# Sources of the first FFN pair kept on chip instead of passing through DRAM

## The chip, the core and the metric

The kernel runs on one core of a Trainium2 chip. That core has five engines that run side by side and wait for each other through semaphores: TensorE (PE in the profile, with its weight loads as PEld), VectorE (DVE), ScalarE (ACT), GpSimd (POOL), and SyncE (SP), which here does nothing but issue DMA transfers, one after the other. Each engine works through its own list of instructions in a fixed order; one that has to wait holds up all that stand behind it on its engine. The metric is the time of one execution on the device, in microseconds.

## The reference

One decoder layer on a sequence of 512 tokens with 2048 features, all float32. The part that matters here is its end:

```
x  = x + mix @ w_out                                  # mix: 512 x 2048, w_out: 2048 x 2048
h2 = rms_norm(x, norm2_g)
x  = x + (silu(h2 @ w_gate) * (h2 @ w_up)) @ w_down   # w_gate, w_up: 2048 x 5632
```

Ahead of it stand a normalisation, one combined projection, gated linear attention on four heads and dilated windowed attention on eight; the change touches none of these.

## The kernel before

**Big products.** Every large product, activations times weights, runs in *pairs* of two output column chunks of 512 columns, by a scheme of seven block products for a two-by-two block product. The left factor is the activations, transposed: for a *group* of 512 input features (two blocks of 256) and the two halves of the tokens there are four blocks, r11, r21 (first feature block, token half 0 and 1) and r12, r22 (second feature block). The seven products of a pair use seven left factors of each group: A11 = r11, S1 = r21 + r22, S2 = S1 - r11, S4 = r12 - S2, S3 = r11 - r21, A12 = r12 and A22 = r22 (the table `COMBO`). A pair has four groups (for 2048 input features), so 28 of these left factors, and it runs P1, P5, P6, P3, P7, P2, P4, four groups each, 28 *groups of matmuls* in all.

**Splits.** A float32 product is made of three products of a shorter float type. Of each left factor ScalarE makes a high part (L161, a cast) and VectorE a low part (L162, source minus high part); this is `Operand.split`. The weights are split in the same way, 128 x 1024 at a time: ScalarE casts `wh` (L331), VectorE subtracts to give `wl` (L335). A group of matmuls is eight matmuls on `wh` and then four on `wl`, all at L358. For P5, P6, P7 and P4 the weights are also sums of two quarters, and VectorE makes the sum in place (L256) two groups ahead. For P1, P3 and P2 there is no sum. `wh` and `wl` have two buffers each, so VectorE can make the `wl` of a group only when the matmuls on the `wl` two groups before are done.

**What sets the order.** `stream` walks all pairs and all groups; in each group it emits the casts and subtractions of the next one or two, its matmuls, and between the `wh` and `wl` matmuls it calls `p.step()`. That call runs due *deferred* work (`later(n, fn)`: n calls from now) and then takes one step of the *background* list, which holds generators that build left factors for later pairs. `paced([...])` gives how many background steps each call takes, in order; past the end of the list it is one. The framework then fixes the order of each engine from dependences, buffers and the order of emission, so the places on the engines are not exactly those of the code.

**From w_out to the FFN.** The second pair of `w_out` makes column chunks 2 and 3 of the new x. Its four closing products give them one token half at a time, in the order P3 (chunk 3, token half 1), P7 (chunk 3, half 0), P2 (chunk 2, half 1), P4 (chunk 2, half 0). `final_out` adds the old x (loaded into tiles `q` and `k`, L1192; added at L1194 or L1197), stores the sum for later (L1211), squares it for the norm (L1213) and defers `turn`, which transposes the tile on TensorE (L1019, eight matmuls of 128 x 128), scales it out of PSUM by norm2_g on ScalarE (L1030) into tiles `oT` and `PT`, and stores these to the DRAM tensors `xn_d` (L1034). The row factor of the norm is applied only when the FFN's products leave PSUM (`tok_scale`).

The first FFN pair (weights `w_gate` and `w_up`, columns of j = 0) takes its left factors for groups 0 and 1 from chunks 0 and 1, and for groups 2 and 3 from chunks 2 and 3. For groups 0 and 1 `operand_jobs` loads the turned blocks back from `xn_d` into tiles `r` (L1073) and splits them during the second `w_out` pair. For groups 2 and 3 `early_job` loads r11 and r21 into tiles `top` (L1073) and makes A11 and S3, and `late_jobs` loads blocks again, into `r` (L1073) and `v`, `T`, `qT`, `kT` (L1107), and makes S1, S2 (L1121, L1123), S4 (L1125), A12 and A22. All these left factors stay in SBUF for the 11 FFN pairs. `before_ffn(0)` makes sure that S3 of group 3 has been emitted before the first FFN pair begins; from there the list `paces[0]` places the steps.

## Time and profile before

| what | value |
|---|---|
| three runs | 1965.07 us median, 1964.33 to 1965.67 |
| the profiled execution's own time | 1958.01 us |
| its span, from the first to the last instruction | 1956.1 us |
| mean granted TensorE clock | 0.999 |
| DMA packets of the execution | 158855, 362.52 MB |
| second `w_out` pair, 28 groups | from 642.12 us |
| first FFN pair, 28 groups | from 720.81 us |

The profile is one execution with the profiler on. Busy times of engines are sums over their instructions; since instructions of one engine overlap a little at their ends, the distance from one start to the next is what a row of instructions costs. In the listing of instructions by time a line gives start, duration, engine, line of the code, operation, the tiles (out<-in, buffer numbers left out), how many equal ones were merged, and in square brackets how long the engine had been idle before and who ended that. SPq is SyncE's list of DMA issues: its durations are those of issuing, not of the transfer.

In what follows W0 to W27 are the groups of matmuls of the second `w_out` pair and F0 to F27 those of the first FFN pair; `wl(F1)` is the low weight part of group F1. Groups 4 to 11, 16 to 19 and 24 to 27 of a pair use summed weights.

### The profile page before, as it was taken

The numbers are of one execution on the slowest core, as the hardware profiler recorded it, in microseconds if no ns is written. First come the engines' busy times: TensorE is split into PE (matmuls) and PEld (weight loads), VectorE is DVE, ScalarE is ACT, GpSimd is POOL, SyncE is SP. The second block draws the span as 40 slices with busy tenths as digits, with TensorE's granted clock in tenths as the row PEclk, the third lists the DMA queues.
The fourth block names the chain that finished last, engine by engine and source line by source line (L and its number), as shares of the span: only waits on it lengthen the run. The fifth ranks groups of instructions, "written<-read, shape, count | busy, mean of one in ns | idle before, by whom it ended". The sixth has DMA issues, their size and how long they took to land.

```text
span 1956.1 us, 25599 instructions
## 1 busy us (share of the span) xinstructions
PE 1918.2 (98%) x9160; PEld 1657.3 (85%) x9160; DVE 1648.0 (84%) x1845; ACT 1088.1 (56%) x1580; POOL 55.2 (3%) x73
## 2 busy tenths in 40 slices
PE   8999999999999999999999999999999999999998
PEld 6788888888878888888888888888888888888887
DVE  7996887768789989878878879879879989989977
ACT  9654554667666665544544545545546646546443
POOL 0000330011000000000000000000000000000000
PEclk9999999999999999999999999999999999999999
DMA  9545555444567584453453453443445865855662
GB/s 355 174 154 206 179 173 171 143 156 162 198 217 241 181 289 148 154 188 141 155 183 135 162 182 120 171 171 124 173 170 176 279 212 182 292 198 180 230 215 76
DMA packets 158855, 362.52 MB, mean 185 GB/s; under 512 B 16438, under 2 KB 43359, under 8 KB 158728
## 3 DMA queue, kind: packets, MB, share of 16 engines
q1 hardware_dynamic: 158584, 360.89, 53.1%
q8 instruction: 71, 1.16, 0.2%
q14 instruction: 56, 0.46, 0.1%
q10 hardware_dynamic: 144, 0.01, 0.0%
HBM read 298.68 MB, written 64.51 MB: 186 GB/s over the span
## 4 chain that ended last, share of the span: by engine, by line
PE 75%; DVE 6%; DMA 3%; issue 2%; ACT 1%; SPq 0%; POOL 0%; DVEq 0%; ACTq 0%
PE acc L358 71%; DVE wl L335 2%; PE bank L1019 1%; DVE wa L256 1%; PE bank L926 1%; PE bank L904 1%; DVE AS L162 1%; PE bank L919 0%; DMA xn_d<-PT 0%; DMA q<-y_d 0%; PE bank L895 0%; DMA q<-in_x 0%; DMA T<-p_d 0%; DMA r<-xn_d 0%; ACT wh L331 0%
## 5 line engine op out<-in xcount | busy, mean ns | idle before, releaser
L358 PE MATMUL acc<-wh,AS 128*128 128x512 f32 x3008 | 712.2, 379 | 0.9 <-DVE AS L162 0.8
L358 PEld LDWEIGHTS acc<-wh,AS 128*128 128x128 f32 x3008 | 568.0, 189 | 82.8 <-DVE AS L162 1.6
L331 ACT CAST wh<-wa 128x1024 fp32r<-128x1024 f32 x376 | 394.3, 1049 | 395.1 <-PE acc L358 365.2
L358 PE MATMUL acc<-wh,AA 128*128 128x512 f32 x2256 | 533.7, 379 | 1.1 <-ACT wh L331 0.9
L335 DVE TENSOR_TENSOR wl<-wa,wh 128x1024 fp32r<-128x1024 f32 x376 | 458.7, 1223 | 74.5 <-ACT wh L331 45.6
L358 PEld LDWEIGHTS acc<-wh,AA 128*128 128x128 f32 x2256 | 426.0, 189 | 62.7 <-ACT wh L331 2.3
L358 PE MATMUL acc<-wl,AS 128*128 128x512 f32 x1504 | 395.3, 385 | 7.6 <-DVE wl L335 7.5
L358 PEld LDWEIGHTS acc<-wl,AS 128*128 128x128 f32 x1504 | 279.2, 189 | 61.0 <-DVE wl L335 20.3
L358 PE MATMUL acc<-wl,AA 128*128 128x512 f32 x1128 | 296.1, 385 | 3.4 <-DVE wl L335 3.3
L358 PEld LDWEIGHTS acc<-wl,AA 128*128 128x128 f32 x1128 | 209.3, 189 | 35.8 <-DVE wl L335 7.5
L331 ACT CAST wh<-wb 128x1024 fp32r<-128x1024 f32 x94 | 98.6, 1049 | 123.8 <-PE acc L358 117.1
L331 ACT CAST wh<-wc 128x1024 fp32r<-128x1024 f32 x94 | 98.4, 1047 | 109.2 <-PE acc L358 106.6
L331 ACT CAST wh<-wd 128x1024 fp32r<-128x1024 f32 x94 | 98.6, 1049 | 103.6 <-PE acc L358 98.5
L335 DVE TENSOR_TENSOR wl<-wc,wh 128x1024 fp32r<-128x1024 f32 x94 | 115.0, 1223 | 41.7 <-ACT wh L331 41.7
L335 DVE TENSOR_TENSOR wl<-wd,wh 128x1024 fp32r<-128x1024 f32 x94 | 114.8, 1223 | 37.8 <-ACT wh L331 28.7
L256 DVE TENSOR_TENSOR wa<-wc,wa 128x1024 f32<-128x1024 f32 x94 | 114.8, 1225 | 35.6 <-DMA wc<-in_w_gate 20.8
L335 DVE TENSOR_TENSOR wl<-wb,wh 128x1024 fp32r<-128x1024 f32 x94 | 114.5, 1221 | 5.3 <-ACT wh L331 4.9
L256 DVE TENSOR_TENSOR wa<-wb,wa 128x1024 f32<-128x1024 f32 x94 | 113.8, 1222 | 1.7 <-DMA wb<-in_w_in 1.0
L256 DVE TENSOR_TENSOR wb<-wd,wb 128x1024 f32<-128x1024 f32 x94 | 114.8, 1223 | 0.4
L256 DVE TENSOR_TENSOR wa<-wd,wa 128x1024 f32<-128x1024 f32 x94 | 113.5, 1223 | 0.1
L298 DVE SCALAR_TENSOR_TENSOR seed<-acc,rs,seed 128x512 f32<-128x512 f32 x96 | 70.5, 747 | 27.6 <-PE acc L358 27.5
L282 ACT ACTIVATE seed<-acc,rs 128x512 f32<-128x512 f32 x96 | 60.8, 682 | 3.1 <-PE acc L358 3.1
(285 smaller groups left out, 1332.2 us busy)
## 6 DMA issues: line engine op xcount, KB each, us to landing
wa<-in_w_gate SPq DMA_DIRECT2D x44, 512.0 KB, 3.4
wb<-in_w_up SPq DMA_DIRECT2D x44, 512.0 KB, 4.0
wd<-in_w_up SPq DMA_DIRECT2D x44, 512.0 KB, 4.1
wc<-in_w_gate SPq DMA_DIRECT2D x44, 512.0 KB, 3.4
wc<-in_w_in SPq DMA_DIRECT2D x28, 512.0 KB, 3.5
wa<-in_w_in SPq DMA_DIRECT2D x24, 512.0 KB, 4.9
wb<-in_w_in SPq DMA_DIRECT2D x24, 512.0 KB, 5.7
wd<-in_w_in SPq DMA_DIRECT2D x24, 512.0 KB, 5.1
```

Of the source, the lines that this page charges most:

```text
L162: nc.vector.tensor_tensor(a[:, :, 1, :], src, a[:, :, 0, :].bitcast(F32), op=ALU.subtract)
L256: nc.vector.tensor_tensor(src, self.quarter(one, g), src, op=ALU.subtract)
L282: nc.scalar.activation(halves(t), unfolded(src[m]), AF.Copy, scale=self.scale(half, m))
L298: nc.vector.scalar_tensor_tensor(halves(seed[m]), unfolded(src[m]), self.scale(half, m), halves(seed[m]), op0=ALU.mult, op1=ALU.add,)
L331: nc.scalar.copy(high[k], sources[k])
L335: nc.vector.tensor_tensor(low[k], sources.pop(k), high[k].bitcast(F32), op=ALU.subtract)
L358: nc.tensor.matmul(p.dst[prod][m], a[:, jj, hl, m * P : (m + 1) * P], folded(w[:, jj, :]), start=fresh and g == 0 and len(terms) == 2 and ...
L904: nc.tensor.matmul(lp[:, :n], qh[:, b * P : (b + 1) * P], kh[:, :n], start=True, stop=True)
L926: nc.tensor.matmul(op, vh[:, k, :], lgs[b][:, k * P : (k + 1) * P], start=(k == 0), stop=(k == b))
L1019: nc.tensor.transpose(bk[:, jj, m * P : (m + 1) * P], tiles[m][:, f : f + P], ident)
```

## The change

Column chunks 2 and 3 no longer go through DRAM on their way to the first FFN pair. In the second `w_out` pair `turn` leaves what ScalarE takes out of PSUM in SBUF: chunk 3 in the tiles `v`, `T` (token half 1) and `qT`, `kT` (half 0), chunk 2 in four tiles `r`. The eight stores to `xn_d` of this pair and the sixteen loads of these blocks are gone, with `early_job` and `late_jobs` for this pair. A new generator `kept_job` makes the left factors of groups 2 and 3 from these tiles in place, in the order of the string `KEPT`: a word `A11.2` is a split, `=S3.2` is the sum S3 of group 2 (written over a kept tile), and words joined by + are one background step. The number of splits and sums is the same as before, 14 and 8. The list `paces[0]` now gives steps to the groups F0 to F3, F10 to F13 and those from F18 on; S3 need no longer be made before the first FFN pair, A11 of group 3 is the last that must. `turn` of the closing product P4 is now deferred by two steps instead of three, in both `w_out` pairs, and in the first pair the background work that hangs on it is appended one step earlier.

```diff
@@ -24,6 +24,7 @@
 DK = 128
 DV = 256
 NB = 640
+KEPT = "A11.2 A11.3 =S3.2+S3.2 =S3.3+S3.3 =S2.2+=S1.2+S1.2 =S2.3+=S1.3+S1.3 S2.2 S2.3 =S4.2+S4.2 =S4.3+S4.3 A12.2 A12.3 A22.2 A22.3"
 PRODUCTS = ("P1", "P5", "P6", "P3", "P7", "P2", "P4")
 UPPER_FIRST = ("P1", "P2", "P5", "P6", "P3", "P7", "P4")
 
@@ -1022,7 +1023,7 @@
             if spare is None:
                 d = work(("oT", "PT")[b], (P, 2, 256))
             else:
-                d = spare[:, b]
+                d = spare[b] if dsts is None else spare[:, b]
             if gains is None:
                 nc.scalar.copy(d, bk)
             else:
@@ -1031,6 +1032,8 @@
                         d[:, jj, :], bk[:, jj, :], AF.Copy,
                         scale=gains[:, 2 * b + jj : 2 * b + jj + 1],
                     )
+            if dsts is None:
+                continue
             store(dsts[b][half], d)
             done.add((id(dsts[b]), half))
 
@@ -1198,6 +1201,33 @@
                 res.append(tiles[m])
         return res
 
+    kept = {}
+
+    def kept_job(op, kept):
+        tt = nc.vector.tensor_tensor
+        sums = {
+            "S3": ("t1", "t0", "t1", ALU.subtract), "S2": ("t1", "r1", "t1", ALU.subtract),
+            "S1": ("t0", "t1", "t0", ALU.add), "S4": ("t1", "r0", "t1", ALU.subtract),
+        }
+        parts = {"A11": "t0", "S3": "t1", "S1": "t0", "S2": "t1", "A12": "r0", "S4": "t1", "A22": "r1"}
+        have = lambda n: (n[0], int(n[1])) in kept
+        for word in KEPT.split():
+            for one in word.split("+"):
+                name, *g = one.split(".")
+                split = name in parts and one[0] != "="
+                name = name.strip("=")
+                g = int(g[0])
+                needs = [parts[name]] if split else sums[name][:3]
+                while not all(have(n) for n in needs):
+                    yield
+                at = lambda n: kept[n[0], int(n[1])][g - 2]
+                if split:
+                    op.split(name, g, at(parts[name]))
+                else:
+                    d, a, b, how = sums[name]
+                    tt(at(d), at(a), at(b), op=how)
+            yield
+
     def final_out(second):
         def final(half, which, tiles, acc_):
             tok = 1 - half
@@ -1216,14 +1246,21 @@
             dsts, gains = xn_d[2 * ch : 2 * ch + 2], g2[:, 4 * ch : 4 * ch + 4]
 
             def turn():
-                transposed_store(tiles, tok, dsts, gains)
-                if not second and which == 0 and half == 1:
-                    background.append(operand_jobs(opn, tops, bots, 0, 2))
-                elif second and which == 1 and half == 1:
-                    background.append(early_job(opn, [(g, tops[g]) for g in (2, 3)], False))
-                    background.append(late_jobs(opn, ((2, 3),), tops, bots, False))
-
-            later(3 if which == 0 and half == 1 else 2, turn)
+                if not second:
+                    transposed_store(tiles, tok, dsts, gains)
+                    if which == 0 and half == 1:
+                        background.append(operand_jobs(opn, tops, bots, 0, 2))
+                        background.append(kept_job(opn, kept))
+                    return
+                if which == 1:
+                    kept["t", tok] = [work(n, (P, 2, 256)) for n in (("qT", "kT"), ("v", "T"))[tok]]
+                else:
+                    kept["r", tok] = [
+                        rpool.tile([P, 2, 256], F32, name=nm("r"), tag="r") for _ in range(2)
+                    ]
+                transposed_store(tiles, tok, None, gains, spare=kept["tr"[which == 0], tok])
+
+            later(2, turn)
             if second and which == 0 and half == 1:
                 for n in range(3):
                     later(1 + n, lambda n=n: output_scales(n))
@@ -1327,10 +1364,10 @@
                 )
         return staged(items, 2)
 
-    paces = {0: [0, 1, 1, 1, 1, 0, 0, 1, 1] + [0] * 6, 10: [0] * 6}
+    paces = {0: [1, 1, 1, 1, 0, 0, 0, 0, 0, 0, 1, 1, 1, 1, 0, 0, 0, 0], 10: [0] * 6}
     def before_ffn(j):
         if j == 0:
-            finish(lambda: ("S3", 3) in opn.t)
+            finish(lambda: ("A11", 3) in opn.t)
         elif j == 10:
             background.append(down_jobs(0))
 
```

VectorE across the start of the first FFN pair, before: the rows from `wl(W27)` to `wl(F1)`. `wa_1147` holds the weights of W27, `wa_1269` those of F0 and `wa_1273` those of F1; `top_1257` and `top_1260` hold the blocks of groups 2 and 3 that came back from DRAM.

```order
L335 TENSOR_TENSOR wl_1270_6585<-wa_1147_5954,wh_1268_6581 128x1024
L215 TENSOR_TENSOR top_1257_6520<-top_1257_6520 128x512
L162 TENSOR_TENSOR AA11_1267_6574<-top_1257_6520,AA11_1267_6574 128x2x256
L215 TENSOR_TENSOR top_1260_6541<-top_1260_6541 128x512
L335 TENSOR_TENSOR wl_1274_6607<-wa_1269_6583,wh_1272_6603 128x1024
L162 TENSOR_TENSOR AS3_1271_6596<-top_1257_6520,AS3_1271_6596 128x2x256
L162 TENSOR_TENSOR AA11_1279_6635<-top_1260_6541,AA11_1279_6635 128x2x256
L162 TENSOR_TENSOR AS3_1280_6643<-top_1260_6541,AS3_1280_6643 128x2x256
L256 TENSOR_TENSOR wa_1269_6583<-wb_1299_6712,wa_1269_6583 128x1024
L335 TENSOR_TENSOR wl_1285_6652<-wa_1273_6605,wh_1283_6648 128x1024
```

The same place now, again from `wl(W27)` to `wl(F1)`: `v` and `T` hold token half 1 and `qT` and `kT` half 0 of chunk 3, `q_1285` is the residual of P4 and `r_1275` a turned block of chunk 2.

```order
L336 TENSOR_TENSOR wl_1270_6582<-wa_1147_5954,wh_1268_6578 128x1024
L163 TENSOR_TENSOR AS3_1267_6571<-v_1233_6398,AS3_1267_6571 128x2x256
L1228 TENSOR_TENSOR T_1234_6399<-kT_1254_6501,T_1234_6399 128x512
L336 TENSOR_TENSOR wl_1274_6604<-wa_1269_6580,wh_1272_6600 128x1024
L163 TENSOR_TENSOR AS3_1271_6593<-T_1234_6399,AS3_1271_6593 128x2x256
L257 TENSOR_TENSOR wa_1269_6580<-wb_1295_6701,wa_1269_6580 128x1024
L1197 TENSOR_TENSOR q_1285_6655<-acc_1137_5920,q_1285_6655 128x512
L1228 TENSOR_TENSOR v_1233_6398<-r_1275_6614,v_1233_6398 128x512
L336 TENSOR_TENSOR wl_1284_6645<-wa_1273_6602,wh_1282_6641 128x1024
```

The splits of A11 have moved up behind `wl(W25)`, nothing in this stretch reads a block that came back from DRAM, and the residual add of P4 (with q_1285) now stands ahead of `wl(F1)`, where it stood behind it.

VectorE a little later, before: the rows behind `wl(F3)` up to `wl(F5)`, whose weights are the sums in `wa_1269` (F4) and `wa_1273` (F5); `r_1293` and `r_1295` are blocks loaded from DRAM and then summed in place.

```order
L1242 SCALAR_TENSOR_TENSOR ms2_153<-ms2_153,rt2_154 128x4
L256 TENSOR_TENSOR wa_1284_6650<-wb_1315_6787,wa_1284_6650 128x1024
L1243 TENSOR_TENSOR ms2_153<-ms2_153,rt2_154 128x4
L1121 TENSOR_TENSOR r_1293_6694<-v_1294_6696,r_1293_6694 128x512
L335 TENSOR_TENSOR wl_1305_6742<-wa_1269_6583,wh_1303_6737 128x1024
L162 TENSOR_TENSOR AS1_1297_6703<-r_1293_6694,AS1_1297_6703 128x2x256
L1121 TENSOR_TENSOR r_1295_6698<-T_1296_6700,r_1295_6698 128x512
L1244 SCALAR_TENSOR_TENSOR rs2_155<-ms2_153,rt2_154 128x4
L1123 TENSOR_TENSOR r_1293_6694<-r_1293_6694,qT_1301_6727 128x512
L256 TENSOR_TENSOR wa_1291_6680<-wb_1321_6814,wa_1291_6680 128x1024
L162 TENSOR_TENSOR AS1_1302_6730<-r_1295_6698,AS1_1302_6730 128x2x256
L335 TENSOR_TENSOR wl_1316_6790<-wa_1273_6605,wh_1314_6785 128x1024
```

The same place now, from `wl(F3)` to `wl(F5)`; `r_1297` is the turned block of group 2 from P4's turn.

```order
L336 TENSOR_TENSOR wl_1296_6704<-wa_1291_6678,wh_1294_6699 128x1024
L163 TENSOR_TENSOR AS2_1301_6732<-T_1234_6399,AS2_1301_6732 128x2x256
L257 TENSOR_TENSOR wa_1273_6602<-wb_1303_6741,wa_1273_6602 128x1024
L336 TENSOR_TENSOR wl_1304_6744<-wa_1269_6580,wh_1302_6739 128x1024
L1279 SCALAR_TENSOR_TENSOR ms2_153<-ms2_153,rt2_154 128x4
L1228 TENSOR_TENSOR v_1233_6398<-r_1297_6714,v_1233_6398 128x512
L1280 TENSOR_TENSOR ms2_153<-ms2_153,rt2_154 128x4
L257 TENSOR_TENSOR wa_1283_6643<-wb_1309_6769,wa_1283_6643 128x1024
L1281 SCALAR_TENSOR_TENSOR rs2_155<-ms2_153,rt2_154 128x4
L163 TENSOR_TENSOR AS4_1305_6758<-v_1233_6398,AS4_1305_6758 128x2x256
L336 TENSOR_TENSOR wl_1310_6772<-wa_1273_6602,wh_1308_6767 128x1024
```

Between these two `wl` five sums and splits of left factors have become three (the split of S2 of group 3, then the sum and the split of S4 of group 2). Two weight sums stand there in both, before those of F6 and F7, now those of F5 and F6. The sums and splits of S1, and those of S2, of both groups now stand ahead of `wl(F4)`.

SyncE at the same time, before: from the first of the `wd` loads for the FFN to the stores of the turned blocks of P2.

```order
L222 DMA wd_1325_6835<-in_w_up 128x1024
L1073 DMA top_1257_6520<-xn_d6_150 128x512
L1073 DMA top_1260_6541<-xn_d7_151 128x512 x2
L1211 DMA x1_d2_142<-seed_1166_6048 128x512
L1211 DMA x1_d3_143<-seed_1172_6074 128x512
L1192 DMA q_1286_6662<-in_x 128x512
L1192 DMA k_1287_6665<-in_x 128x512
L1107 DMA qT_1301_6727<-xn_d6_150 128x512
L1107 DMA kT_1310_6773<-xn_d7_151 128x512
L222 DMA wd_1328_6854<-in_w_up 128x1024
L1034 DMA xn_d4_148<-oT_1276_6622 128x512
L1034 DMA xn_d5_149<-PT_1278_6631 128x512
```

Now: from the first of the `wd` loads for the FFN to the stores of P4's sums.

```order
L223 DMA wd_1317_6811<-in_w_up 128x1024
L223 DMA wd_1320_6830<-in_w_up 128x1024
L223 DMA wd_1323_6849<-in_w_up 128x1024
L1241 DMA x1_d2_142<-seed_1168_6053 128x512
L1241 DMA x1_d3_143<-seed_1174_6080 128x512
L1195 DMA q_1285_6655<-in_x 128x512
L1195 DMA k_1286_6658<-in_x 128x512
L223 DMA wd_1327_6870<-in_w_up 128x1024
L1241 DMA x1_d0_140<-q_1285_6655 128x512
L1241 DMA x1_d1_141<-k_1286_6658 128x512
```

The loads for P4's residual (`q_1285`, `k_1286`) now stand behind three weight loads and two stores, and no issue there waits for a turned block to be stored or to land.

## The prediction

> **What bounds the kernel now.** I read first the busy times of the page, then the listing of matmuls between the start of the second `w_out` pair and the end of the first FFN pair, then who waited for whom there, then the listings of VectorE, ScalarE and SyncE at the waits. The first line below is the page's busy times; the next three are waits of PE and DVE between 719 and 760 us and 716 and 760 us (total, times, longest); the last three are busy times by stretch (PE, PEld, DVE, ACT, POOL, granted clock, DMA share, GB/s).
>
> ```profile
> PE 1918.2 (98%) x9160; PEld 1657.3 (85%) x9160; DVE 1648.0 (84%) x1845; ACT 1088.1 (56%) x1580; POOL 55.2 (3%) x73
> ...
> PE acc L358 <- DVE wl L335: 5.4, 5, 1.8
> ...
> DVE top L215 <- DMA top<-xn_d: 4.9, 2, 3.1
> ...
> DVE r L1121 <- DMA r<-xn_d: 0.7, 1, 0.7
> ...
> 652.00:680.50 28.50, 27.81 (x126) 22.42 (x124) 28.42 (x33) 19.60 (x30) 0.00 (x0) 1.00 0.31 102
> ...
> 700.00:720.00 20.00, 20.00 (x102) 17.50 (x101) 13.91 (x18) 10.97 (x20) 0.00 (x0) 1.00 0.96 334
> 720.00:757.07 37.07, 31.54 (x144) 25.67 (x143) 34.51 (x44) 26.00 (x44) 0.00 (x0) 1.00 0.56 189
> ```
>
> TensorE bounds the kernel: it is busy 98% of the span, so all a change in order can win is its idle time. Around the change that idle time lies in 720 to 757 us, where PE waits five times for a `wl`, and VectorE, which makes it, had stood 4.9 us idle for blocks that came back from DRAM. In the 20 us ahead of it VectorE was busy only 13.91, with the DMA engines at 96%. How much TensorE loses is read from the starts in its listing (start, duration, what).
>
> ```profile
> 708.36 1.11 PE L358 MATMUL acc<-wl,AA 128*128 128x512 f32 x4
> 709.30 1.89 PE L358 MATMUL acc<-wh,AA 128*128 128x512 f32 x8
> ...
> 717.07 1.89 PE L358 MATMUL acc<-wh,AA 128*128 128x512 f32 x8
> ...
> 719.59 1.11 PE L358 MATMUL acc<-wl,AA 128*128 128x512 f32 x4
> 720.81 2.00 PE L358 MATMUL acc<-wh,AA 128*128 128x512 f32 x8
> 724.30 1.13 PE L358 MATMUL acc<-wl,AA 128*128 128x512 f32 x4 [1.49 <-DVE wl L335]
> 725.27 1.89 PE L358 MATMUL acc<-wh,AA 128*128 128x512 f32 x8
> 728.38 1.13 PE L358 MATMUL acc<-wl,AA 128*128 128x512 f32 x4 [1.22 <-DVE wl L335]
> ...
> 737.99 1.89 PE L358 MATMUL acc<-wh,AS 128*128 128x512 f32 x8
> 741.67 1.13 PE L358 MATMUL acc<-wl,AS 128*128 128x512 f32 x4 [1.79 <-DVE wl L335]
> ...
> 750.44 1.89 PE L358 MATMUL acc<-wh,AS 128*128 128x512 f32 x8
> 752.63 1.13 PE L358 MATMUL acc<-wl,AS 128*128 128x512 f32 x4 [0.30 <-DVE wl L335]
> 753.60 1.89 PE L358 MATMUL acc<-wh,AS 128*128 128x512 f32 x8
> 756.11 1.13 PE L358 MATMUL acc<-wl,AS 128*128 128x512 f32 x4 [0.62 <-DVE wl L335]
> 757.07 1.89 PE L358 MATMUL acc<-wh,AS 128*128 128x512 f32 x8
> 758.80 1.03 PE L358 MATMUL acc<-wl,AS 128*128 128x512 f32 x4
> 759.66 1.89 PE L358 MATMUL acc<-wh,AS 128*128 128x512 f32 x8
> ```
>
> Undisturbed, eight `wh` matmuls take 1.73 us (757.07 to 758.80) and four `wl` 0.86 (to 759.66), 2.59 a group; with a tile's transposes between them the `wl` start 2.52 after the group (717.07 to 719.59) and take 0.94 (708.36 to 709.30), 3.46 in all. What goes beyond that is lost: 0.28 ahead of F0 (720.81 - 719.59 - 0.94), then 1.76, 1.38, 1.95, 0.46 and 0.78 ahead of five `wl`, and 0.11 behind each of them (724.30 to 725.27 is 0.97, not 0.86). The sum is 7.2 us, and it is the ceiling of what this place can give.
>
> **The removed transfers.** Eight stores and sixteen loads of 256 KB go, with their places in SP's row. On the path they were the waits of VectorE above: L215 for `top` and L1121 for `r`. The `top` loads could be issued only when the turned blocks had landed:
>
> ```profile
> 716.67 1.48 SPq L1073 DMA_DIRECT2D top<-xn_d  x3
> ...
> 719.15 0.47 SPq L1192 DMA_DIRECT2D q<-in_x  x1
> ```
>
> The DMA engines themselves are no path here (56% in the stalled stretch), so the freed traffic is worth nothing by itself. Splits and sums are as many as before on ACT and DVE: 0.
>
> **The turn one step earlier, first `w_out` pair.** The rows of DVE change places between 652 and 680 us, where it is busy 28.42 of 28.50 us and TensorE loses a little to it; the largest piece is here.
>
> ```profile
> 680.56 1.13 PE L358 MATMUL acc<-wl,AS 128*128 128x512 f32 x4 [0.62 <-DVE wl L335]
> ```
>
> Between the `wl` of W4 and that of W13 DVE has the same set of rows in both kernels, only in another order. A full engine with the same rows ends at the same time, so I take 0. The ends: this stall of 0.8 gone (−0.8), and an equal one added (+0.8); the middle is nearest, as DVE has no idle time to give.
>
> **The sources kept on chip: VectorE's path through F0 to F5.** The durations of its rows come from this listing.
>
> ```profile
> 709.90 1.22 DVE L335 TENSOR_TENSOR wl<-wa,wh 128x1024 fp32r<-128x1024 f32 x1
> ...
> 719.25 0.69 DVE L215 TENSOR_TENSOR top<-top 128x512 f32<-128x512 f32 x1 [3.08 <-DMA top<-xn_d]
> ...
> 722.42 0.69 DVE L215 TENSOR_TENSOR top<-top 128x512 f32<-128x512 f32 x1 [1.87 <-DMA top<-xn_d]
> ...
> 727.10 1.22 DVE L335 TENSOR_TENSOR wl<-wa,wh 128x1024 fp32r<-128x1024 f32 x1
> 728.24 0.68 DVE L1194 TENSOR_TENSOR q<-acc,q 128x512 f32<-128x512 f32 x1
> 728.84 0.68 DVE L1194 TENSOR_TENSOR k<-acc,k 128x512 f32<-128x512 f32 x1
> 729.44 1.22 DVE L335 TENSOR_TENSOR wl<-wa,wh 128x1024 fp32r<-128x1024 f32 x1
> 730.57 0.17 DVE L1236 TENSOR_REDUCE ms<-ss 128x4 f32<-128x16 f32 x1
> 730.65 1.22 DVE L256 TENSOR_TENSOR wa<-wb,wa 128x1024 f32<-128x1024 f32 x1
> ```
>
> From start to start a `wl` or a weight sum takes 1.14 us (big), a split, sum or residual add 0.60 (small), a row of the norm 0.08. I walk the new order with these from `wl(W25)` at 709.90, which stands where it stood. It ends at 711.04; three small and `wl(W26)`: 713.98; three small and `wl(W27)`: 716.92; two small and `wl(F0)`: 719.26; one small and the sum for F4: 721.00. Then come the residual add on `q` (P4's matmuls end at 719.59 + 1.11 = 720.70, in time) and the first S2 sum: 722.20; `wl(F1)` 723.34; five small and `wl(F2)` 727.48; two small, two of the norm and `wl(F3)` 729.98; one small, a weight sum and `wl(F4)` 732.86; two small, three of the norm, a weight sum and `wl(F5)` 736.58, with its last 0.09 of duration 736.67.
>
> TensorE without stalls starts F0 at 720.53, F1 at 723.12, F2 at 725.71 (now with the transposes), F3 at 729.17, F4 at 731.76, F5 at 734.35, and wants the `wl` of F1 to F5 at 724.85, 728.23, 730.90, 733.49 and 736.08. So all are in time but that of F5, 0.59 late; with 0.11 for the restart TensorE loses 0.7. Behind it a group with a summed weight needs 2.28 of 2.59 us on DVE, and those without (F10 to F13) have room for the splits put there: nothing more is lost.
>
> **What else stands in that path.** ScalarE must have the turned block of P2 for the S2 sum at 721.60.
>
> ```profile
> 708.73 0.82 ACT L1030 ACTIVATE oT<-bank,g 128x256 f32<-128x256 f32 x2
> ...
> 719.71 1.05 ACT L331 CAST wh<-wa 128x1024 fp32r<-128x1024 f32 x1
> ```
>
> Its `wh(F1)` can start when the `wh` matmuls of W27 are done, about 719.0, takes 1.0, and two scalings take 0.82: 720.8, in time. The ends are 0 and 0.6 (late by a small row); I take 0. The residual load `q` is the unknown: it now stands ahead of `wl(F1)` on DVE, and its issue behind the two stores of the sums that DVE has ready at 714.67 and 715.27 (two of the three small ahead of `wl(W27)`); with 0.47 an issue it goes out at 715.7. How long such a load takes (KB and median; then shortest, median, longest of all in_x loads):
>
> ```profile
> q<-in_x SPq DMA_DIRECT2D x8, 256.0 KB, 5.3
> ...
> DMA to landing us min/median/max: 3.1/5.8/10.2
> ```
>
> It lands between 718.8 (no wait) and 725.9 (4.9 us late); by the two medians 721.0 and 721.5, and I take 0.3 late. The Trainium skill ("DMA: Bandwidth & Descriptors", "Anatomy of one DMA — SWDGE (gpsimd) path") gives some 2.0 us plus the bytes at 436 GB/s, by which I estimate 2.6 us and no wait (1958.6 instead of 1958.9); no in_x load of the trace was so short.
>
> **Sum.** −7.2 + 0.7 + 0.3 = −6.2 us. Against the profiled execution's own 1958.01 us that is 1951.8. The runs' median stands 7.06 above that execution, and I take the same difference from it: 1965.07 − 6.2 = **1958.9**.
>
> **Rivals.** *The residual comes late.* For: 700 to 720 us has the DMA engines at 96%, and three weight loads now go out ahead of `q`. Against: three of the removed loads went out in the same 20 us (at 716.67), with the stores that they waited for ahead of them. At the longest landing the loss is 0.7 + 4.9, the gain 1.6: 1963.5. *DVE's instructions do not overlap.* If each cost its whole duration, 0.09 more, the 14 rows to `q` and the 24 from there to `wl(F5)` would make it 38 x 0.09 = 3.4 later, a gain of 2.8 and 1962.3. Against: a `wl` of 1.22 us at 727.10 and the next start at 728.24. The Trainium skill ("VectorE: DVE Perf Modes", "The DRAIN you can't avoid") says just that, the next operation does not start until the pipe is empty; by this row it does start 0.08 ahead of the former's end. *Slower.* VectorE's add on `q` holds up every later `wl`, so a late load costs its whole lateness. The gain is used up when `q` lands 6.5 us after 721.0, 11.8 us after its issue, and the kernel is 4 us slower (1969) at 15.8. For: the load waits behind `wd` loads that themselves wait for DVE's `wl(W26)`. Against: 10.2 was the longest seen, in a busier stretch.
>
> **How the numbers follow.** A measurement of this kernel tells about 0.2% (3.9 us) from no change. The forecast, 1957.5 to 1960.5 with the first pair's turn and a `q` up to 1.5 us late, has 0.70; the late residual, 1960.5 to 1969, has 0.18, of which 0.03 lies under 1961.1; no overlap on DVE 0.04; the slower rival 0.08, of which 0.01 stays within the 0.2%. So faster 0.73, within 0.2% 0.15 + 0.04 + 0.01 = 0.20, slower 0.07. The range 1957.5 to 1963.5 leaves out the slower case and the latest landings, under 2 in 10; its lower end is the full 7.2 with the runs' own spread.
>
> **What would show it.** Right: no L215 rows in 700 to 760 us, DVE busy without a wait for DMA from 711 to 737 us, one PE wait of about 0.5 us ahead of the `wl` of F5, F12 starting near 753.5 instead of 759.66. Wrong: DVE idle ahead of the adds on `q` (L1197) by more than 1 us, or PE waits for `wl` in F1 to F4 or behind F5.

## The result, and the profile after

The changed kernel takes **1956.9 us** (median of six runs, 1954.17 to 1960.89) against 1965.02 us of the kernel before on the same chip (six runs, 1962.77 to 1966.78): ratio 0.996, 95% interval 0.9948 to 0.9972, a gain of 8.1 us in an interval of about 5.5 to 10.2. The forecast was 1958.9 us in 1957.5 to 1963.5: right in direction, but the measured time lies 0.6 us under the lower end of its range. One execution of the kernel before in a later set took 2885.86 us at a granted clock of 0.655, where the others had 0.995 or more; it is in none of the figures here.

The profiled execution of the changed kernel took 1960.89 us, the slowest of the six; that of the kernel before, at 1958.01 us, was faster than any of its timed runs. Their spans (1959.1 and 1956.1 us) therefore say the opposite of the medians, and the two traces can be compared only place by place. First TensorE through the first FFN pair of the changed kernel (start, duration, what, and what ended a wait):

```profile
723.59 1.89 PE L359 MATMUL acc<-wh,AA 128*128 128x512 f32 x8
...
727.06 1.89 PE L359 MATMUL acc<-wh,AA 128*128 128x512 f32 x8
...
735.02 1.13 PE L359 MATMUL acc<-wl,AA 128*128 128x512 f32 x4
735.99 1.89 PE L359 MATMUL acc<-wh,AA 128*128 128x512 f32 x8
...
740.38 1.13 PE L359 MATMUL acc<-wl,AS 128*128 128x512 f32 x4
741.35 1.89 PE L359 MATMUL acc<-wh,AS 128*128 128x512 f32 x8
744.08 1.13 PE L359 MATMUL acc<-wl,AS 128*128 128x512 f32 x4 [0.83 <-DVE wl L336]
745.04 1.89 PE L359 MATMUL acc<-wh,AS 128*128 128x512 f32 x8
...
760.58 1.89 PE L359 MATMUL acc<-wh,AS 128*128 128x512 f32 x8
```

723.59 is W27 and 760.58 is F12: 36.99 us, where the kernel before took 42.59 (717.07 to 759.66). So **5.6 us are gained in place**, of a loss that was 7.2. What is left is 1.56 us: `wl(F2)` 0.18 late behind its transposes, `wl(F4)` 0.08, `wl(F5)` 1.00, and 0.10 behind each. The waits of VectorE in 700 to 770 us (total, times, longest) and its rows:

```profile
DVE seed L295 <- PE acc L359: 1.5, 1, 1.5
DVE q L1197 <- DMA q<-in_x: 0.8, 1, 0.8
DVE wl L336 <- ACT wh L332: 0.6, 1, 0.6
```

```profile
716.42 1.22 DVE L336 TENSOR_TENSOR wl<-wa,wh 128x1024 fp32r<-128x1024 f32 x1
...
726.37 1.22 DVE L257 TENSOR_TENSOR wa<-wb,wa 128x1024 f32<-128x1024 f32 x1
728.40 0.69 DVE L1197 TENSOR_TENSOR q<-acc,q 128x512 f32<-128x512 f32 x1 [0.82 <-DMA q<-in_x]
...
729.61 1.22 DVE L336 TENSOR_TENSOR wl<-wa,wh 128x1024 fp32r<-128x1024 f32 x1
...
742.81 1.22 DVE L336 TENSOR_TENSOR wl<-wa,wh 128x1024 fp32r<-128x1024 f32 x1
```

The waits on `top` and `r` are gone; the one left on a transfer is the residual `q`, 0.82 us. From `wl(W25)` (716.42) to the start of `wl(F5)` (742.81) are 26.39 us; the walk of the prediction had 25.54 without that wait, so 25.57 of 26.39 are as walked. The residual went out when it was to (715.7 + 6.5 = 722.2), but took 6.2 us:

```profile
714.30 6.62 SPq L223 DMA_DIRECT2D wd<-in_w_up  x3
721.20 0.93 SPq L1241 DMA_DIRECT2D x_d<-seed  x2
722.18 0.45 SPq L1195 DMA_DIRECT2D q<-in_x  x1
```

**A second place.** Ahead of W0 and behind the first FFN pair the two kernels do the same work, and executions differ there by themselves, here against the change: the changed kernel is 6.6 us later at W0 (648.71 against 642.12) and takes 5.0 us more from F12 to the last `w_down` pair. One difference goes the other way: that last pair. Kernel before, TensorE and the add on VectorE that it waits for; then the changed kernel:

```profile
1896.28 1.89 PE L358 MATMUL acc<-wh,AA 128*128 128x512 f32 x8
1898.75 1.13 PE L358 MATMUL acc<-wl,AA 128*128 128x512 f32 x4 [0.58 <-DVE wl L335]
...
1924.48 1.89 PE L358 MATMUL acc<-wh,AS 128*128 128x512 f32 x8
```

```profile
1896.87 0.69 DVE L1194 TENSOR_TENSOR q<-acc,q 128x512 f32<-128x512 f32 x1 [2.87 <-DMA q<-y_d]
```

```profile
1902.18 1.89 PE L359 MATMUL acc<-wh,AA 128*128 128x512 f32 x8
...
1928.08 1.89 PE L359 MATMUL acc<-wh,AS 128*128 128x512 f32 x8
```

```profile
1900.24 0.69 DVE L1197 TENSOR_TENSOR q<-acc,q 128x512 f32<-128x512 f32 x1 [0.34 <-DMA q<-y_d]
```

Ten groups take 25.90 us undisturbed (10 x 2.59): the changed kernel lost nothing there, the kernel before 2.30, since its load `q<-y_d` came 2.87 us late. Added to 5.6 that makes 7.9. Whether this belongs to the change is one of the questions of the runs.

### The profile page after: what moved, and what is told of

Its sections match the earlier page's. It is cut to its first block, busy times and chain, and to the rows that moved or that the text cites. A ratio compares the mean times of both kernels' runs of the same rounds, so it can differ in the third digit from the quotient of the medians.

```text
span 1959.1 us, 25566 instructions
## 1 busy us (share of the span) xinstructions
PE 1921.9 (98%) x9160; PEld 1662.6 (85%) x9160; DVE 1648.2 (84%) x1845; ACT 1088.8 (56%) x1580; POOL 49.3 (3%) x73
## 3 DMA queue, kind: packets, MB, share of 16 engines
q8 instruction: 72, 1.18, 0.3%
## 4 chain that ended last, share of the span: by engine, by line
PE 73%; DVE 7%; DMA 3%; issue 2%; ACT 1%; POOL 0%; SPq 0%; DVEq 0%; ACTq 0%
PE acc L359 69%; DVE wl L336 3%; DVE wa L257 1%; PE bank L1020 1%; DVE AS L163 1%; PE bank L927 1%; PE bank L905 1%; DMA wc<-in_w_in 0%; PE bank L920 0%; PE bank L896 0%; DMA kT<-S_d 0%; DVE wb L257 0%; DMA v<-S_d 0%; DMA xn_d<-oT 0%; DMA q<-in_x 0%
```

## The experiments

All runs in one table. "First FFN" is what TensorE loses from W27 to F12 beyond 35.43 us (42.59 less the 7.16 counted in the kernel before), "last pair" what it loses in the ten groups above beyond 25.90. Both come from the one profiled execution of each run, as differences of listed starts (good to 0.01); the medians come from the timed ones, beside the kernel before on the same chip.

```text
run                first FFN  last pair   median (runs)    before then
before             7.16       2.30        1965.02 (6)
after              1.56       0.00        1956.90 (6)      1965.02
e2_before_again    7.05       2.73        1963.80 (11)     1964.08
e12_before_third   8.41       1.18        1962.26 (11)     1963.66
e1_after_again     2.15       0.13        1956.36 (6)      1964.08
e11_after_third    1.55       0.50        1957.03 (7)      1963.66
e7_old_paces       1.30       0.83        1956.95 (5)      1964.08
e8_turn2           7.67       2.41        1965.44 (12)     1965.26
e3_stores_back     2.26       2.24        1958.02 (6)      1965.26
e4_resid_own       0.66       0.59        1955.98 (6)      1965.26
e5_s4_later        1.12       0.78        1957.49 (6)      1965.26
e6_both            0.20       0.15        1956.93 (6)      1964.08
e9_b8              7.62       1.22        1963.74 (10)     1963.43
e9_b16             7.31       2.23        1964.59 (10)     1963.43
e9_a8              2.01       1.25        1955.66 (4)      1963.43
e9_a16             1.58       0.56        1955.24 (5)      1963.43
e10_f1             1.07       1.30        1957.14 (10)     1962.32
e10_f2             6.61       0.67        1960.80 (10)     1962.32
e10_f3             0.98       0.96        1955.66 (4)      1962.32
e10_f4             0.94       1.36        1957.44 (3)      1962.32
```

**How much is it, and where? Both kernels repeated, unchanged.**

> The changed kernel once more, unaltered. Theory 1 (the gain lies only between W27 and F12, where the profile of the changed kernel has matmuls 5.6 us earlier relative to W27; all else in the medians is variation of stretches that run the same instructions): 5.6 us faster than the kernel before, 4 to 7. Theory 2 (the removed transfers also shorten other stretches by 2.5 us, as the first medians, 8.1 us apart, suggest): 8 us faster. In its profile both expect the matmuls from W27 to F12 to gain 5 to 6.5 us on the profile of before, by how late the residual load lands.

> The kernel before, unaltered, handed in as a variant, so that it shows what two equal kernels differ by. Both theories: no difference, within 1.5 us in the median. Theory 1 also expects its profile to differ from the first one by several us in the stretches that depend on DMA landings (ahead of 640 us, and behind 1600 us) and by under 1 us between W0 and F12 outside the waits for blocks from DRAM; theory 2 expects less than 2 us of such difference.

> The changed kernel unchanged. If the difference in the last w_down pair belongs to the kernels, the stretch takes 27.6 to 28.0 us as in the other two profiles, and the timed runs are 7 to 8 us below the kernel before: 5.0 to 5.6 in the first FFN pair and 2.2 here. If it is scatter, the stretch can take anything from 27.6 to 30.4 us, and the gain by the runs is nearer 5.5. In the first FFN pair W27 to F12 takes 34.4 to 35.0 us.

> The kernel before unchanged. If the difference belongs to the kernels, the last w_down pair's stretch takes 29.9 to 30.4 us again; if it is scatter, anything from 27.6. W27 to F12 takes 39.9 to 40.0 us. Time that of the kernel before within 0.1%.

The ratios were 0.9965 (0.9952 to 0.9977), 1.0002 (0.9991 to 1.0012), 0.9964 (0.995 to 0.9978) and 0.9996 (0.9987 to 1.0004). In the three sets of runs that hold both, the mean of the changed kernel's runs lies 7.7, 7.6 and 6.3 us under that of the kernel before. Single runs of one kernel scatter with a standard deviation of 2.2 us, so the mean of the three, 7.2 us, is known to about 1.2: **6.0 to 8.4 us**. In the first FFN pair the three profiles of each kernel lose 7.54 and 1.75 us in the mean: 5.8 gained. In the last pair 2.07 and 0.21: 1.9 more, and from there to the end of the span another 0.7 (31.67 against 30.95 us).

The places do not add up to the timed gain, though. In the same six profiles the changed kernel is 4.1 us later at W0 in the mean (647.8 against 643.7) and takes 3.1 us more from F12 to the last pair (1139.9 against 1136.8), so that its spans are only 1.6 us shorter. Over the seven profiles of each kind that are set against each other at the end of this section these two shrink to 1.7 and 1.2, with single profiles of one kind up to 9 and 5 us apart. So neither theory of the first expectation is settled: the 5.6 us of theory 1 lie just under the timed 6.0 to 8.4, the 8 of theory 2 inside it, and that the 1.9 us are a part of the timed gain is not shown.

The third profile of the kernel before is the instructive one. It lost more than the others in the first FFN pair, since its `top` blocks came later still, and less than they in the last:

```profile
DVE top L215 <- DMA top<-xn_d: 6.5, 2, 4.5
```

So neither place has a fixed price: each hangs on a load that arrives about when it is needed, and what it costs moves by 1.4 and 1.6 us over three executions. The expectation of 29.9 to 30.4 us for the last stretch in that run (the ten groups and the `wh` matmuls behind them; it took 28.81) failed; the changed kernel's 28.13 lay just above its 27.6 to 28.0. The figures that these two expectations give for W27 to F12 are one group of 2.59 us short and fit W27 to F11: so read, the changed kernel took 34.4 us as expected, and the kernel before 41.3 where 39.9 to 40.0 were expected, the same late blocks.

**Which part of the change carries the gain?** First the kept sources with the splits placed as before; then the earlier turn alone, in the kernel before. This edit moves the turn of P4 in both `w_out` pairs, as the change does, and not in the first alone, as its expectation has it.

```diff
 # e7_old_paces, against the changed kernel
-    paces = {0: [1, 1, 1, 1, 0, 0, 0, 0, 0, 0, 1, 1, 1, 1, 0, 0, 0, 0], 10: [0] * 6}
+    paces = {0: [0, 1, 1, 1, 1, 0, 0, 1, 1] + [0] * 6, 10: [0] * 6}
...
-            finish(lambda: ("A11", 3) in opn.t)
+            finish(lambda: ("S3", 3) in opn.t)
```

> The changed kernel with the list of paces and the condition ahead of the first FFN pair as they were before: the sources stay on chip, the splits lie in the old places. Theory K (keeping the sources is what gains; the placing hardly matters): walking VectorE's row, the low weight part of F5 is in time, those of F6 and F10 come 0.8 and 0.4 us late, and the loss between W27 and F12 is 1.3 to 2.2 us against 1.6, so 5 to 6 us faster than before. Rival (placing gains what the three late parts in F5, F9 and F10 cost before, 3.5 us with their restarts): the loss is about 5 us, and the kernel only 2 us faster than before.

```diff
 # e8_turn2, against the kernel before
-            later(3 if which == 0 and half == 1 else 2, turn)
+            later(2, turn)
```

> The kernel before, with one edit of the change alone: the turn of the first w_out pair's blocks goes out two steps later instead of three. Theory 1 (all of the gain lies in the first FFN pair): the first pair's stretch to W0 moves by no more than 0.5 us either way, W27 to F12 loses 7.0 to 7.5 us as before, time 1964.2 +-1.2. Theory 2 (the 2 us by which the medians differ beyond the gain in place come from this edit): 1962 to 1962.5, and a stretch between 640 and 720 us is 1 to 2 us shorter.

With the old placement the waits only change places: `wl(F6)` and `wl(F10)` are late instead of F2, F4 and F5, and the loss is 1.30 us, at first sight less than 1.56. But the residual came only 0.35 us late in this profile (the last line below), against 0.82. With the new placement and a residual 0.33 late (e10_f1, further down) the loss is 1.07, so at equal lateness the new placement is some 0.2 us ahead.

```profile
741.33 1.13 PE L359 MATMUL acc<-wl,AS 128*128 128x512 f32 x4 [0.51 <-DVE wl L336]
...
752.22 1.13 PE L359 MATMUL acc<-wl,AS 128*128 128x512 f32 x4 [0.26 <-DVE wl L336]
```

```profile
723.39 0.69 DVE L1197 TENSOR_TENSOR q<-acc,q 128x512 f32<-128x512 f32 x1 [0.35 <-DMA q<-in_x]
```

The turn alone gives nothing (ratio 1.0001, 0.9992 to 1.0011; the loss of 7.67 is a little over the 7.0 to 7.5 expected): its stretch from 642 us to W27 was 0.7 us shorter in that profile, but in other kernels with the old turn it lay between 0.8 shorter (e9_b8) and 0.4 longer (e12). So the kept sources carry the gain in place but for some 0.2 us, and the new placement is worth nothing that shows in the timed runs.

**The wait, or the traffic?** The changed kernel with the eight stores made again, and still no loads.

```diff
-            if dsts is None:
+            if kept_in is not None:
+                store(kept_in[b][half], d)
                 continue
...
-                transposed_store(tiles, tok, None, gains, spare=kept["tr"[which == 0], tok])
+                transposed_store(tiles, tok, None, gains, spare=kept["tr"[which == 0], tok], kept_in=dsts)
```

> The changed kernel, but the eight stores of the turned blocks of the last two column chunks to xn_d are made again (2.1 MB written, never read; the loads stay away). Theory W (only the waits of VectorE for blocks read back counted): from W27 to F12 TensorE loses what it loses in the changed kernel, 1.6 to 2.2 us instead of 7.2, since four of the stores go out on SP ahead of the residual q but their blocks are ready by then, and the other four behind it; the time is that of the changed kernel, 1956.5 +-1.3. Rival T (the freed traffic and SP's row are worth something of their own, the 2 us by which the medians differ beyond the 5.0 to 5.6 us read in place): q lands later by about as long as four more stores take, 0.5 to 1.5 us, or the stretches elsewhere lose more, and the time is 1958 to 1959.

The loss in the first FFN pair is 2.26 us, of the size of the repeat's 2.15, and again it is the residual:

```profile
728.79 0.69 DVE L1198 TENSOR_TENSOR q<-acc,q 128x512 f32<-128x512 f32 x1 [1.52 <-DMA q<-in_x]
```

It went out at 721.87, so its landing took 6.9 us; in the ten profiles without the stores and with the residual in the same tiles it took 5.6 to 6.8. The ratio, 0.996 (0.9946 to 0.9973), is that of the changed kernel. The median by itself, 1958.02, lies outside theory W's 1956.5 +-1.3 and at the edge of T's 1958 to 1959, but the kernel before was slower on that chip too (1965.26). Theory W holds for the first FFN pair: the eight stores show no cost there beyond what the residual scatters by itself, and what counted was that VectorE waited for the blocks to come back. The traffic of the sixteen loads was not put back without their waits, so for the loads this is read from the waits that are gone, not tested. But in the last pair this kernel lost 2.24 us, like the kernel before; that is followed up below.

**The residual and the fifth group.** P4's residual in tiles that are free earlier; the sum S4.2 with its split put off to F10; and both.

```diff
 # e4_resid_own
-            r = work(("q", "k")[m])
+            r = work(tags[m])
...
+                ("oT", "PT") if second and tiles is None else ("q", "k"),
 # e5_s4_later
-    paces = {0: [1, 1, 1, 1, 0, 0, 0, 0, 0, 0, 1, 1, 1, 1, 0, 0, 0, 0], 10: [0] * 6}
+    paces = {0: [1, 1, 1, 0, 0, 0, 0, 0, 0, 0, 1, 1, 1, 1, 0, 0, 0, 0], 10: [0] * 6}
```

> The changed kernel, with P4's residual loaded into the tiles oT and PT, which are free earlier, instead of q and k, so its load does not wait for the two stores of sums ahead of it. Theory L (the late residual is the whole of what the walk had mis-sized): VectorE has no wait for a DMA ahead of the residual add, wl(F5) starts 0.8 to 1.4 us earlier than in the changed kernel's two profiles, the PE waits ahead of wl of F1, F2 and F4 go and that of F5 falls from 1.00 to 0 to 0.3 us; loss from W27 to F12 0.1 to 0.6 us, in place 1.1 to 2 us better than the changed kernel, time 1955 to 1956 by the medians, which the spread of runs hardly tells from 1956.5. Rival P (the placement of the splits makes F5 late by itself): the wait at F5 stays at 0.6 us or more and the loss at 0.7 or more.

> The changed kernel, with the fourth of the early entries of paces (the sum S4.2 with its split) put off to the group F10, and the residual left as it is. Theory L: the wait for q stays (0.3 to 1.4 us, by the run), so F2 and F4 stay 0 to 0.7 us late, F5 has 1.2 us of VectorE's work less ahead of it and is in time or 0.1 late, and F10, which now has one more sum and split, is about 0.5 us late; loss from W27 to F12 0.7 to 1.5 us, at best 0.9 better than the changed kernel, time 1955.5 to 1956.5. Rival P: the wait at F5 goes and nothing takes its place, loss under 0.4.

> The changed kernel with two further edits: P4's residual is loaded into the tiles oT and PT, which are free there, so that its load need not wait for the tiles q and k; and the sum and split of S4 of group 2 move from the fourth background step of the first FFN pair to the steps in F10 to F13. Walking VectorE's row with the measured distances: the add on the residual no longer waits 0.8 us, the low weight part of F5 is 1.2 us earlier still and in time, that of F10 is about 0.3 us early. So the loss between W27 and F12 falls from 1.6 us to at most 0.3, the kernel is 7 us faster than before, 1.4 faster than the changed one. If VectorE is not what delays F5, the loss stays above 1 us.

In e4 VectorE has no wait for the residual any more, the waits at F2 and F4 are gone, and one is left, 0.56 us ahead of `wl(F5)` (0.40 on PE and the rest on its weight load):

```profile
725.37 0.68 DVE L1197 TENSOR_TENSOR oT<-acc,oT 128x512 f32<-128x512 f32 x1
```

```profile
741.04 1.13 PE L359 MATMUL acc<-wl,AS 128*128 128x512 f32 x4 [0.40 <-DVE wl L336]
```

That is the 0.59 us which the walk gave for the new placement by itself: neither form of the expectation was exact, for L had this wait at 0.3 at most and P at 0.6 or more. So, by the difference of these two profiles, the 1.56 us of the changed kernel are 0.66 from the placement and 0.90 from a residual 0.82 late. In e5 the residual's wait of 0.8 stays, F5 is in time, and F10, which got the work, is late by 0.46, all as its theory L had it:

```profile
756.02 1.13 PE L359 MATMUL acc<-wl,AS 128*128 128x512 f32 x4 [0.30 <-DVE wl L336]
```

With both the loss is 0.20 us, the lowest of all. Against the changed kernel these are 0.4 to 1.4 us by the profiles, which the timed runs cannot tell: the medians of the three are 1955.98, 1957.49 (1 us over what was expected) and 1956.93 (beside 1956.36 of the changed kernel on the same chip, where 1.4 less was expected), and the ratios 0.9954 (0.994 to 0.9968), 0.9958 (0.9946 to 0.997) and 0.9964 (0.9951 to 0.9977).

**The last pair.** First theory C, that the number of transfers issued before carries over: extra stores of `p_d` blocks to a scratch tensor in the kernel before (b) and the changed one (a), 8 or 16 of them.

```diff
             store(dsts[b][half], d)
+            if pad is not None:
+                store(pad[b], d)
...
-                transposed_store(up, half, p_d[2 * j : 2 * j + 2])
+                pad = pads[2 * half + 4 * (j - 3) :] if j in (3, 4) else None
+                transposed_store(up, half, p_d[2 * j : 2 * j + 2], pad=pad)
```

> The kernel before, with eight more stores of 256 KB in the FFN pairs 3 and 4 (the p_d blocks written a second time, to a scratch tensor nobody reads, near 900 to 1100 us where SyncE and the DMA engines have room). What it is for: in the last w_down pair the residual load q<-y_d landed 5.6 to 6.9 us after its issue in the four profiles of kernels with 24, 24, 24 and 8 of the removed and restored transfers (before, its repeat, the earlier turn, the stores back), and TensorE lost 1.9 to 2.8 us there; in the six profiles without any of them it landed 3.9 to 5.2 us after and TensorE lost 0 to 0.9, though the order of work there is the same with 8 stores as with none. Theory C (the number of transfers issued so far, by its remainder by 16, carries over): this kernel issues 8 more than before, the remainder of the changed kernel, so the loss in the last pair falls from 2.0 to 2.8 us to under 1. Rival R (what carries over is whether the scratch xn_d of those chunks is in use): the loss stays at 1.9 to 2.8 us.

> The changed kernel, with the same eight extra stores in the FFN pairs 3 and 4. Theory C: its count of transfers is that of the kernel with the stores back, so the last w_down pair loses 1.9 to 2.8 us again instead of 0 to 0.9. Rival R: it stays at 0 to 0.9 us. In the first FFN pair both expect what the changed kernel lost, 1.6 to 2.2 us.

> The kernel before, with sixteen extra stores (FFN pairs 3 to 6). Theory C: the remainder by 16 is that of the kernel before, so the last w_down pair loses 2.0 to 2.8 us as there. Rival R: the same. If eight extra stores help and sixteen don't, the count carries it; if both help, it is something the stores themselves do.

> The changed kernel, with sixteen extra stores (FFN pairs 3 to 6). Theory C: the remainder by 16 is that of the changed kernel, so the last w_down pair loses 0 to 0.9 us. Rival R: the same. If it loses 1.9 us or more, any added store at all brings the loss back, and neither holds. First FFN pair: 1.6 to 2.2 us.

The last pair lost 1.22, 1.25, 2.23 and 0.56 us. The sixteens are as both theories had them; the eights lie between the two, and e9_a8 and e3, with the same count, lost 1.25 and 2.24. C falls, and so does R in the form that it was put, by which e9_b8 had to lose 1.9 or more.

Then theory A, the place in DRAM: it takes it that with `xn_d` of the last chunks unused the tensors behind it lie 2 MB lower, which no view of the profile shows. A scratch tensor of 2 MB (f1, f2, f3) or 4 MB (f4) with a single store is to move them again, first used in the first FFN pair, or in the last one (f3); f2 is the kernel before, the others the changed one.

```diff
+    pad_d = dram([8, P, 2, 256], "pad_d")
...
+            if pad is not None and b == 0:
+                store(pad[0], d)
...
-                transposed_store(up, half, p_d[2 * j : 2 * j + 2])
+                transposed_store(
+                    up, half, p_d[2 * j : 2 * j + 2], pad=pad_d if (j, half) == (0, 0) else None
+                )
```

> The changed kernel with a scratch tensor of 2 MB, into which one store of 256 KB goes in the first FFN pair and which nobody reads: p_d from its second tensor on, the sums and y_d lie where they lie in the kernel before, 2 MB higher than in the changed one. Theory A (place in DRAM): the residual load q<-y_d in the last w_down pair lands late as before and TensorE loses 2.0 to 2.8 us there; time about 2 us above the changed kernel, 1958.5. Rival (place plays no part): 0 to 0.9 us lost there, time 1956.6.

> The kernel before with the same scratch tensor and store: everything behind it another 2 MB higher. Theory A, in the form that places 4 MB apart behave alike (what the eight and sixteen extra stores left possible): the last w_down pair loses 0 to 1.2 us instead of 2.3 to 2.7, time about 1962.5. Rival: 2.0 to 2.8 us lost there, time 1964.3.

> The changed kernel with the scratch tensor of 2 MB used first in the last FFN pair, so that only the last sums and y_d lie 2 MB higher. Theory A with y_d's place as the cause: 2.0 to 2.8 us lost in the last w_down pair. Theory A with the places of p_d or the sums as the cause, or the rival: 0 to 0.9 us.

> The changed kernel with a scratch tensor of 4 MB and one store in the first FFN pair. Theory A in the form that places 4 MB apart behave alike: 0 to 0.9 us lost in the last w_down pair. If it loses 2 us or more, any higher place does it; if e10_f1 loses nothing too, place plays no part.

The losses were 1.30, 0.67, 0.96 and 1.36 us. e10_f1, which was to have the later tensors where the kernel before has them, lost neither 2 us nor under 0.9, and e10_f3 and e10_f4 lie over the 0.9 that was left to them. Only e10_f2 came out as A had it (under 1.2), and against its rival (2.0 or more). A isn't shown, and with the third profile of the kernel before at 1.18 such differences are within what one kernel does in several executions: one profile of each kernel cannot decide ranges this narrow. What remains is a difference of means: seven profiles of kernels with all of the traffic through `xn_d` (the kernel before three times, e8, e9_b8, e9_b16, e10_f2) lost 1.8 us there (the least, e10_f2, 0.67); seven without it and without extra stores (the changed kernel three times, e4 to e7) 0.4, none of these over 0.83; the six changed kernels with some extra store or place 1.3. What carries this some 1,200 us further on **stays open**.

## Why the prediction was wrong, and where it was right

**The ceiling of the first FFN pair (7.2 us)** was right for the execution that it was read from, and is no constant: other profiles of the same code there (in e8 but for the turn) lost 6.6 to 8.4 us (kernel before, e8, e9_b8, e9_b16, e10_f2), as the `top` blocks happened to land.

**The walk of VectorE** was right to 0.03 us in 26 us, its start-to-start prices of 1.14 and 0.60 us with it, and so was the 0.59 us at `wl(F5)` (0.56 in e4). With them falls the rival of instructions that do not overlap; the paragraph of the Trainium skill that the prediction names for it ("VectorE: DVE Perf Modes", "The DRAIN you can't avoid") itself ends by saying that an operation that is not held starts earlier, as these rows do. That nothing is lost behind F5 held; of F1 to F4, which were to be in time, F2 and F4 were 0.18 and 0.08 late through the residual, one of the signs that the prediction named for being wrong.

**The residual** was mis-sized: 0.3 us late by the prediction, 0.82, 1.40 and 0.8 in the three profiles of the changed kernel (the 1.40 is put down to PE there, whose matmuls of P4 had ended 1.8 us earlier; more than 1 us was another of the signs). It landed 6.2, 6.8 and 6.2 us after its issue, not 5.3. The three e10 kernels with the changed order had it 0.2 to 0.3 late, so the prediction's value is one that occurs, only not in these. Each 0.1 us costs about 0.1, as the prediction had it for the slower rival: 0.82 late cost 0.90, 1.40 cost 1.49 (2.15 less 0.66). The prediction's estimate from the Trainium skill ("DMA: Bandwidth & Descriptors", "Anatomy of one DMA — SWDGE (gpsimd) path"), 2.6 us and no wait, was further off than the medians of the rows; that section is on transfers issued from GpSimd, and this load is issued by SyncE.

**The earlier turn (0)** held by e8, and **the removed traffic in this place (0)** by e3 as far as the stores go.

**In place**, then, the sum of 6.2 us became 5.6, since the residual cost 0.90 us instead of 0.3, and 5.8 over three profiles of each. That error goes the other way from the miss. What failed are the two steps after it. The first is "I take the same difference from it", with the sum of one pair taken as that of the whole kernel: every other stretch was put at nothing without a reason. A second load that arrives about when it is needed, `q<-y_d` in the last `w_down` pair, was not in the sum, and there the changed kernel lost 1.9 us less over three profiles of each; why it does stays open, and so does how much of it is in the timed gain. The second is the range, "its lower end is the full 7.2 with the runs' own spread": it took the ceiling of one place in one execution for that of the kernel, and the spread of three runs (1.3 us) for the runs' own, which is 6.7 us over six runs of one kernel; and its chances add up to 1 without any for a time under 1957.5.

Part of the miss is the draw of the runs. The gain over all runs, 7.2 us (6.0 to 8.4), takes in the forecast's 6.2, and with 7.2 the time would have been 1957.8, inside the range; the first six runs of the changed kernel came out at 8.1.

## What to carry to other kernels

Keep on chip what the next stage reads at once: here leaving out the round trip won 5.8 us in the first FFN pair, the bytes of the stores alone cost nothing that shows, and the order in which the parts were then made was worth some 0.2 us. Where VectorE has no idle time and its work stands behind a load, as in the first FFN pair here, that load's lateness goes to TensorE nearly one to one, so give it a tile that is free early (here 0.9 us). And size a forecast by place, but its range by the scatter of the runs: a loss that hangs on a load landing in time is a distribution, of which one profile shows one draw.

## What the runs showed of the hardware that was not expected

Two executions of the same program differ by several microseconds in all, much of it ahead of the stretches compared here (W0 began at 642 to 651 us in the twenty profiles), and in the two places looked at closely by when a transfer lands. The last `w_down` pair lost 2.30, 2.73 and 1.18 us in three executions of the kernel before; the `top` blocks of 256 KB cost VectorE 4.9, 4.5 and 6.5 us of waiting in the same three.
